# The down projection of a gated MLP: seven products over 14 of 22 k tiles instead of 12, and another order of the last row's tail

## The chip, the cores and the metric

The kernel runs on one core of one Trainium2 chip. The metric is the device time of one execution in microseconds. All arithmetic is in float32: every matrix is split into a high and a low float32r part, and a product of two matrices is three TensorE products (high by high, high by low, low by high), accumulated in PSUM.

## The reference

One decoder block for 512 tokens and 16 meta tokens, model width 1024. Two mixers (an HGRN2 recurrence and a Mamba-2 scan) read one input projection, and one output projection joins them. A gated MLP follows, with a causal convolution of width 3 between the up projection and the activation, and a final RMSNorm:

```python
def conv_glu_ffn(h, w_up, conv_w, conv_b, w_down):
    u = causal_dwconv(h @ w_up, conv_w, conv_b)
    gate, val = jnp.split(u, 2, axis=-1)
    return (jax.nn.silu(gate) * val) @ w_down      # 2816 -> 1024
...
        h = h + conv_glu_ffn(rmsnorm(h, norm2_w[l]), ffn_w_up[l], ...)
    y = rmsnorm(h, final_norm_w)
    return y[:, N_META:, :]
```

The change touches only the last product, `(silu(gate) * val) @ w_down`, and the final norm behind it.

## The kernel before

Activations are held transposed: 128 features on the partitions, tokens along the free axis. The down projection has 22 k tiles (`acs[0..21]`, the gated activations, split into `ah` and `al`) and 8 output row tiles `j` of 128 features, each 512 tokens wide. Row tiles 0 and 1 are plain products (tile `pdn`, lines 1172 to 1174). Row tiles 2 to 7 come in three pairs, `p` = 1, 2, 3, with `j = 2p` and `j2 = 2p + 1`.

Within a pair, `DK` = 6 k tiles from `D0` = 8 on, and the 6 behind them, are multiplied by the scheme of seven products on 2 x 2 blocks: the blocks of the weights are (row j or j2) by (first or second group of k tiles), those of the activations are (group of k tiles) by (first or second 256 tokens). Seven products of `DK` k tiles and 256 columns take the place of eight. The sums of weights that it needs (`sumsdn`) are made by accumulating DMAs on POOL's queue, long before for pairs 1 and 2, and during the plain rows for pair 3. The sums of activations (`gated_sums(i)`: four operations on VectorE, two splits, each of them one on ScalarE and one on VectorE; tiles `g13`, `g24`, then `g0h`, `g0l`, `g1h`, `g1l`) are made while the plain rows run.

The products go by keys, and each has its weight tile of the same name (`whi_d_1` is the high part of a product of pair 1):

- `d0`, `d1`: into `x`, the first 256 tokens of row j. After `d0`, ScalarE copies `x` into `y` (line 1199; PSUM tile `psn2_0`, called `psn` in the trace).
- `d2`: into `y`. Then ScalarE copies `y` into `z`, the second 256 tokens of row j, in the same PSUM tile `pup` as `x` (line 1207).
- `d3`: into `v` (tile `pv`), copied to `ds7` (line 1210).
- `d5` into `z`, `d6` into `y`; `ds7 + z` and `ds7 + y` are then subtracted from row j2.
- `d4`: into `z`.
- The k tiles outside of the scheme, plainly: `qa` (8 tiles) and `qb` (2 tiles) for row j2, `ra` and `rb` for row j; in pair 3 the first half's share is taken earlier as `xa` and `xb`.

Each weight tile goes through three steps: a DMA on SP's queue into `raw`, a ScalarE copy into `whi` (line 203), a VectorE subtraction into `wlo` (line 204). There are three buffers of each. A ScalarE copy waits until TensorE has done with the buffer's tile before. The copies between PSUM tiles stand in the same ScalarE queue.

The order on each engine is set when the program is built, by a scheduler that takes the ready instruction of highest priority in its own estimate of time; `evac()` and `first()` raise priorities, `tc.issue_after` forbids an instruction to stand ahead of another. On the chip, each engine then runs its list in order.

At the end, row 6 (`end`) is finished in halves of 256 tokens: residual added (line 1241), squared (1242), summed over features by two products with a matrix of ones (1245 for the seven earlier rows in `facc`, 1246 for row 6), logarithm and exponential for the reciprocal root (1247, 1248), eight multiplications on VectorE (1253, 1255) and four output DMAs (1257).

Of the kernel before, what the change touches and what calls it, by code (L numbers as in the profile page):

```python
# [43 lines left out]
C_FN = C_FB + 44  # L44
# [8 lines left out]
SPLITS = {7: (0,), 8: (1, 2), 10: (3,), 13: (4,), 15: (5,), 18: (6,), 21: range(7, 22)}  # L53
WS = [j for j in range(KF) if KINDS[j] == "W"]
DN = 1, 2, 3
D0, DK = 8, 6
GROUPS = WS[0:4], WS[4:8], WS[8:12], WS[12:], [("dn", 1), ("dn", 2)], [("dn", 3)]
HT = 258
NUNSC = 5
# [5 lines left out]
def tile_block(ctx: ExitStack, tc: tile.TileContext, xT, w_in, w_dt, w_out, w_up, w_down,  # L65
               par, consts, consti, out, dbg=None):
    nc = tc.nc
    V, A, G, PE = nc.vector, nc.scalar, nc.gpsimd, nc.tensor

    cp = ctx.enter_context(tc.tile_pool(name="cp", bufs=1))  # L70
# [7 lines left out]
    def slot(name, n=NT, dtype=F32, parts=P, tag="m"):  # L78
        return gp.tile([parts, n], dtype, tag=tag, name=name, bufs=TAGS[tag])
# [39 lines left out]
    with first(300000):  # L119
        w = A.activation(warm[:], eps[:], AF.Copy)  # L120
# [47 lines left out]
    chunks += [dn(j, *p) for p in PARTS for j in range(2)]  # L168
    def dn_chunks(p):

        j, j2, c1, c2, c3 = 2 * p, 2 * p + 1, D0 * P, (D0 + DK) * P, (D0 + 2 * DK) * P

        def summed(n):
            return lambda: sumd["dn", p][:, n * DK * P:(n + 1) * DK * P]

        rest = [(("ra", p), w_down[j][:, 0:c1], D0), (("rb", p), w_down[j][:, c3:], KF - D0 - 2 * DK)]
        r = [(("qa", p), w_down[j2][:, 0:c1], D0), (("d0", p), w_down[j][:, c1:c2], DK),
             (("qb", p), w_down[j2][:, c3:], KF - D0 - 2 * DK), (("d1", p), w_down[j][:, c2:c3], DK), (("d2", p), summed(0), DK),
             (("d3", p), summed(2), DK), (("d5", p), summed(1), DK), (("d6", p), w_down[j2][:, c2:c3], DK)]
# [154 lines left out]
    with first(200000):  # L334
        for k in range(0, KD, 2):
            d = slice(k * P, (k + 2) * P)
            for j, w, kx in ((BT, starts[0], k), (CT, starts[1], k + 1)):
                t = slot(f"x{kx}", tag="y")
# [8 lines left out]
        for k in range(KD):  # L347
# [3 lines left out]
            tag = "b0" if k < 4 else "b1"  # L351
# [5 lines left out]
    with first(190000):  # L357
# [18 lines left out]
    with first():  # L376
        for n, (a0, a1) in enumerate(((0, HALF), (HALF, NT))):
            p = bank(f"psn{n}")
# [4 lines left out]
        for k in range(KD):  # L383
            t = slot(f"xn{k}")
# [44 lines left out]
    for n, (a0, a1) in enumerate(((0, HALF), (HALF, NT))):  # L429
        p = bank(f"psd{n}")[0:66, :]  # L430
# [469 lines left out]
    hs, u2h, u2l = [], [], []  # L900
    pos = {}
    acc = None
    for j, s in oorder:
        w = weights("out", j, s)
# [13 lines left out]
        with evac():  # L918
            sq = slot(f"hsq{j}", tag="pr")
# [227 lines left out]
    def partial(ps, w, xs, start=False, stop=False):  # L1147

        for k, (xh, xl) in enumerate(xs):
            wh, wl = (t[:, k * P:(k + 1) * P] for t in w)  # L1150
            one, end = start and k == 0, stop and k == len(xs) - 1
            PE.matmul(ps, wh, xh, start=one, stop=False, skip_group_check=True)  # L1152
            PE.matmul(ps, wh, xl, start=False, stop=False, skip_group_check=True)  # L1153
            PE.matmul(ps, wl, xh, start=False, stop=end, skip_group_check=True)  # L1154
# [31 lines left out]
    whole, K2, KR = slice(0, 512), D0 + DK, D0 + 2 * DK  # L1186
    end = 2 * DN[-1]
    for p in DN:
        j, j2 = 2 * p, 2 * p + 1
        q = bank(f"pq{p}")  # L1190
        partial(q[:], weights("qa", p), gated(0, D0, whole), start=True)
        xz, was = product_banks(True)
        assert was
        other = product_banks(True)[0] if j == end else xz
        x, z, y, v = xz[:, first_half], other[:, 512:768], u1[0][:, first_half], bank(f"pv{p}")[:, first_half]
        sv, s7 = slot(f"dsv{p}", 512, tag="ab"), slot(f"ds7{p}", 256, tag="rs")
# [3 lines left out]
        partial(q[:], weights("qb", p), gated(KR, KF - KR, whole), stop=True)  # L1200
        V.tensor_tensor(hs[j2][:, META:], hs[j2][:, META:], q[:], ALU.add)
        partial(x, weights("d1", p), gated(K2, DK, first_half))
        if j == end:
            partial(x, weights("xb", p), gated(KR, KF - KR, first_half))
        partial(y, weights("d2", p), [t[1] for t in dts])
        with evac():
            A.activation(z, y, AF.Copy)
        partial(v, weights("d3", p), [t[2] for t in dts], start=True, stop=True)
        with evac():
            A.activation(s7[:], v, AF.Copy)  # L1210
# [20 lines left out]
        others(*([] if j == end else [(x, first_half)]), (z, second_half))  # L1231
        if j < end:
            V.tensor_tensor(by_bank(hs[j][:, META:]), by_bank(hs[j][:, META:]), by_bank(xz[:])[:, :, first_half], ALU.add)
            squares(j)
            continue
        hh, halves, ps = hs[j], (0, 256), {0: x, 256: z}
        sq = slot(f"fsq{j}", 512, tag="pr")
        for d0 in halves:
            d, dh = slice(d0, d0 + 256), slice(META + d0, META + d0 + 256)
            with evac():  # L1240
                V.tensor_tensor(hh[:, dh], hh[:, dh], ps[d0], ALU.add)
                A.activation(sq[:, d], hh[:, dh], AF.Square)
                p = bank(f"psn3_{d0}")
                rs = slot(f"rs{d0}", 256, tag="u")
                PE.matmul(p[:, 0:256], ones, acc[:, d], start=True, stop=False)
                PE.matmul(p[:, 0:256], ones, sq[:, d], start=False, stop=True)
                A.activation(rs[:], p[:, 0:256], AF.Ln, bias=eps[:], scale=1.0 / DM)
                A.activation(rs[:], rs[:], AF.Exp, scale=-0.5)
                for k in range(0, KD, 2):
                    ot = slot(f"ot{d0}_{k}", 512, tag="u")[:].rearrange("p (a t) -> p a t", a=2)  # L1250
                    for i in range(2):
                        if k + i == end:
                            V.scalar_tensor_tensor(ot[:, i, :], hh[:, dh], col(C_FN + j), rs[:], ALU.mult, ALU.mult)
                        else:
                            V.tensor_tensor(ot[:, i, :], hs[k + i][:, dh], rs[:], ALU.mult)
                    dst = out[k * P:(k + 2) * P, d].rearrange("(a p) t -> p a t", p=P)
                    (nc.scalar if k % 4 else nc.sync).dma_start(dst, ot)
# [65 lines left out]
```

## Time and profile before

| | |
|---|---|
| median of 3 runs | 864.2 us (863.01 to 865.95) |
| the profiled execution | 863.18 us, its span 861.3 us |
| granted TensorE clock, mean | 0.997 |
| TensorE busy | 842.8 us, 98% of the span |
| VectorE, ScalarE, GpSimd busy | 612.0, 485.9, 117.8 us |
| plain rows 0 and 1 | about 733 to 763 us |
| pairs 1, 2, 3 | about 763 to 792, 792 to 821, 821 to 850.9 us |
| end of the last large product to the end of the span | 850.9 to 861.3 us |

Times in the trace are counted from the span's start. A row of the timeline gives start, duration, engine, line, operation, output<-inputs, and in brackets the idle time ahead of it with what ended it. A TensorE row lasts longer than the distance to the next one, since matmuls overlap; that distance is what one costs. Buffer numbers and the digits in keys are left out in the trace, so all of `whi_d0` to `whi_d6` read `whi_d`.

### The profile page before, as it was taken

How to read it: one execution, taken by the hardware profiler on the slowest of the kernel's cores; microseconds unless marked ns; L12 is line 12 of the kernel's file. 1: busy time of each engine (PE TensorE's matmuls, PEld its weight loads, DVE VectorE, ACT ScalarE, POOL GpSimd, SP SyncE). 2: the span in 40 equal slices, each digit the busy share in tenths (PEclk: the TensorE clock that was granted, in tenths of full speed). 3: DMA queues.
4: the chain of work that ended last, by engine and by line, in shares of the span. 5: the costliest groups of instructions: out<-in, count | busy, mean ns of one | idle time of the engine just before them, and what ended most of it. 6: DMA issues, size and time to landing. Idle time of an engine off the chain costs nothing. (4 is left out here: it accounts for less than half of the span.)

```text
span 861.3 us, 16951 instructions
## 1 busy us (share of the span) xinstructions
PE 842.8 (98%) x6908; PEld 813.4 (94%) x6908; DVE 612.0 (71%) x1040; ACT 485.9 (56%) x777; POOL 117.8 (14%) x156
## 2 busy tenths in 40 slices
PE   7999999999999999999999999999999999999995
PEld 7998899999999999999999999999999999889995
DVE  7983988798766666645244459888888888984544
ACT  8636986867444544454243244567677667663442
POOL 1321022232223131302211220000000000100000
PEclk9999999999999999999999999999999999999998
DMA  7598378893979597957989992355555555945553
GB/s 250 200 250 216 94 253 203 169 152 103 277 141 183 155 281 140 187 145 244 343 164 215 204 168 78 99 171 182 189 190 184 174 177 167 229 114 154 148 150 108
DMA packets 60142, 156.14 MB, mean 181 GB/s; under 512 B 6280, under 2 KB 10760, under 8 KB 60064
## 3 DMA queue, kind: packets, MB, share of 16 engines
q1 hardware_dynamic: 36704, 98.37, 35.0%
q0 software_dynamic: 20832, 53.09, 31.4%
q10 hardware_dynamic: 2528, 3.60, 1.3%
q8 instruction: 54, 0.88, 0.4%
q14 instruction: 24, 0.20, 0.1%
HBM read 152.89 MB, written 55.23 MB: 242 GB/s over the span
## 5 line engine op out<-in xcount | busy, mean ns | idle before, releaser
L326 PE MATMUL pj<-u_hi,whi_in 128*128 128x272 f32 (+1 forms) x752 | 156.6, 288 | 0.0
L326 PE MATMUL pj<-u_lo,whi_in 128*128 128x272 f32 (+1 forms) x752 | 156.6, 287 | 0.0
L326 PE MATMUL pj<-u_hi,wlo_in 128*128 128x272 f32 (+1 forms) x752 | 155.5, 286 | 0.0
L326 PEld LDWEIGHTS pj<-u_hi,whi_in 128*128 128x128 f32 x752 | 115.9, 188 | 2.8 <-issue 2.7
L326 PEld LDWEIGHTS pj<-u_lo,whi_in 128*128 128x128 f32 x752 | 116.0, 188 | 2.4 <-issue 1.8
L326 PEld LDWEIGHTS pj<-u_hi,wlo_in 128*128 128x128 f32 x752 | 116.3, 189 | 1.4 <-issue 1.3
L204 DVE TENSOR_TENSOR wlo_in<-raw_in,whi_in 128x1024 fp32r<-128x1024 f32 (+1 forms) x58 | 64.3, 1108 | 51.2 <-ACT whi_in L203 51.1
L203 ACT ACTIVATE whi_in<-raw_in 128x1024 fp32r<-128x1024 f32 (+1 forms) x58 | 56.0, 966 | 64.1 <-PE pj L326 58.9
L203 ACT ACTIVATE whi_w<-raw_w 128x1024 fp32r<-128x1024 f32 x54 | 57.1, 1058 | 26.4 <-PE pup L1056 13.3
L204 DVE TENSOR_TENSOR wlo_w<-raw_w,whi_w 128x1024 fp32r<-128x1024 f32 x54 | 65.9, 1220 | 6.4 <-ACT whi_w L203 5.8
L221 POOL COPY tick<-ticks 128x1 f32<-128x1 f32 x6 | 9.2, 1537 | 316.0 <-DVE ticks L220 316.0
L1056 PE MATMUL psn<-t1l,whi_w 128*128 128x258 f32 x144 | 40.9, 284 | 0.0
L1057 PE MATMUL pup<-n_hi,wlo_w 128*128 128x258 f32 x144 | 40.7, 283 | 0.1
L1055 PE MATMUL pup<-n_hi,whi_w 128*128 128x258 f32 x144 | 40.8, 283 | 0.0
L1057 PE MATMUL psn<-t1h,wlo_w 128*128 128x258 f32 x144 | 40.7, 282 | 0.0
L1056 PE MATMUL pup<-n_lo,whi_w 128*128 128x258 f32 x144 | 40.6, 282 | 0.0
L204 DVE TENSOR_TENSOR wlo_d<-raw_d,whi_d 128x768 fp32r<-128x768 f32 x21 | 20.1, 957 | 28.7 <-ACT whi_d L203 28.6
L1055 PE MATMUL psn<-t1h,whi_w 128*128 128x258 f32 x144 | 40.4, 280 | 0.0
L241 POOL DMA_DIRECT2D sums<-in_w_up_dram x18 | 21.2, 1179 | 111.2 <-issue 104.9
L204 DVE TENSOR_TENSOR wlo_out<-raw_out,whi_out 128x1024 fp32r<-128x1024 f32 x16 | 19.6, 1225 | 23.5 <-ACT whi_out L203 23.5
L203 ACT ACTIVATE whi_d<-raw_d 128x768 fp32r<-128x768 f32 x21 | 17.8, 847 | 30.7 <-PE pup L1153 14.3
L203 ACT ACTIVATE whi_out<-raw_out 128x1024 fp32r<-128x1024 f32 x16 | 16.9, 1057 | 26.7 <-PE pout L326 16.2
(474 smaller groups left out, 2563.7 us busy)
## 6 DMA issues: line engine op xcount, KB each, us to landing
sums<-in_w_up_dram POOLq DMA_DIRECT2D x54, 512.0 KB, 8.4
raw_in<-in_w_in_dram SPq DMA_DIRECT2D x50, 512.0 KB, 5.4
sums<-in_w_up_dram POOLq DMA_DIRECT2D x36, 256.0 KB, 8.3
raw_w<-in_w_up_dram SPq DMA_DIRECT2D x18, 512.0 KB, 3.5
raw_w<-sums SPq DMA_DIRECT2D x18, 512.0 KB, 3.7
raw_out<-in_w_out_dram SPq DMA_DIRECT2D x16, 512.0 KB, 6.7
sumsdn<-in_w_down_dram POOLq DMA_DIRECT2D x9, 768.0 KB, 8.9
sums<-sums POOLq DMA_DIRECT2D x18, 256.0 KB, 6.8
```

What stands on the lines that cost most here:

```text
L203: A.activation(hi[:, d], raw[:, d], AF.Copy)
L204: eng.tensor_tensor(lo[:, d], raw[:, d], hi[:, d].bitcast(F32), ALU.subtract)
L221: gate = G.tensor_copy(tick[:], ticks[:, n:n + 1])
L241: G.dma_start(ds[j][:, 0:2], of[j][3], accum_op=ALU.add)
L326: PE.matmul(ps[:, O + a0:O + a1], w, x[:, a0:a1], start=s, stop=e)
L1055: PE.matmul(ps, wh, xh, start=first, stop=False, skip_group_check=True)
L1056: PE.matmul(ps, wh, xl, start=False, stop=False, skip_group_check=True)
L1057: last_product[:] = [PE.matmul(ps, wl, xh, start=False, stop=k == H - 1, skip_group_check=True)]
```

## The change

`DK` is 7 instead of 6, so that the scheme takes k tiles 8 to 21, all behind the first 8. `qb`, `rb` and `xb` disappear. `d0` now stands ahead of `qa`. Row j2 gets three subtractions (`ds7` on both halves, then `z` and `y`, each right behind its product) in place of two additions and one subtraction. A seventh `gated_sums` reads `acs[14]` and `acs[21]`; its buffers come from other pools, and `ds7` has one of its own. In the tail, pair 3's `ra` products for the second half are held behind the first half's product of ones with row 6's squares (`normed`).

```diff
-D0, DK = 8, 6
+D0, DK = 8, 7
...
-        if p == DN[-1]:
-            r[6:8] = r[7], r[6]
-            xa, xb = [(key, *rest[n][1:]) for n, key in enumerate((("xa", p), ("xb", p)))]
-            r[4:4], r[9:9] = [xb], [xa]
-        return r + [(("d4", p), summed(3), DK)] + rest
+        last = [(("d4", p), summed(3), DK), (("ra", p), w_down[j][:, 0:c1], D0)]
+        if p == DN[-1]:
+            d5, d6 = d6, d5
+            last.insert(0, (("xa", p), w_down[j][:, 0:c1], D0))
+        return [(("d0", p), w_down[j][:, c1:c2], DK), (("qa", p), w_down[j2][:, 0:c1], D0), (("d1", p), w_down[j][:, c2:], DK),
+                (("d2", p), summed(0), DK), (("d3", p), summed(2), DK), d5, d6] + last
...
-    places = iter(["b1"] * 6 + ["L"] * 4 + ["u"] * 14)
+    places = iter(["b1"] * 6 + ["L"] * 4 + ["u"] * 12 + ["ab", "pr", "u", "pr", "u", "rs"])
...
+        V.tensor_tensor(by_bank(row2), by_bank(row2), s7[:].unsqueeze(1).broadcast_to([P, 2, 256]), ALU.subtract)
         for key in ("d6", "d5") if j == end else ("d5", "d6"):
-            if key == "d5":
-                partial(z, weights(key, p), [t[0] for t in dts])
-            else:
-                partial(y, weights(key, p), [t[3] for t in dts], stop=True)
-        with evac():
-            V.tensor_tensor(sv[:, second_half], s7[:], z, ALU.add)
-            V.tensor_tensor(sv[:, first_half], s7[:], y, ALU.add)
-        V.tensor_tensor(hs[j2][:, META:], hs[j2][:, META:], sv[:], ALU.subtract)
+            ps, n, d = (z, 0, second_half) if key == "d5" else (y, 3, first_half)
+            partial(ps, weights(key, p), [t[n] for t in dts], stop=key == "d6")
+            with evac():
+                V.tensor_tensor(row2[:, d], row2[:, d], ps, ALU.subtract)
...
         if j == end:
             partial(x, weights("xa", p), gated(0, D0, first_half), stop=True)
         partial(z, weights("d4", p), gated(K2, DK, second_half))
...
+            if d0:
+                with tc.issue_after(normed.ins):
+                    partial(z, weights("ra", DN[-1]), gated(0, D0, second_half), stop=True)
             V.tensor_tensor(hh[:, dh], hh[:, dh], ps[d0], ALU.add)
```

What the scheduler makes of it is seen at three places.

TensorE in pair 1, after the change, from the end of `d3` (tile `pv1`) on. `psn2_0` is `y`, `pup0` holds `z`; `g1h_6` and `g1l_6` are of the seventh sums of activations.

```order
L1150 MATMUL pv1_9323<-g0h_6_9134,whi_d3_1_9385 128x256
L1151 MATMUL pv1_9323<-g0l_6_9135,whi_d3_1_9385 128x256
L1152 MATMUL pv1_9323<-g0h_6_9134,wlo_d3_1_9386 128x256
L1150 MATMUL psn2_0_6080<-g1h_6_9138,whi_d2_1_9354 128x256
L1151 MATMUL psn2_0_6080<-g1l_6_9139,whi_d2_1_9354 128x256
L1152 MATMUL psn2_0_6080<-g1h_6_9138,wlo_d2_1_9355 128x256
L1150 MATMUL pup0_6048<-g0h_0_9050,whi_d5_1_9412 128x256
```

The last three products of `d2` stand behind all of `d3`, directly ahead of `d5`. Before the change all of `d2` stands ahead of `d3`:

```order
L1152 MATMUL psn2_0_6080<-g1h_5_9124,whi_d2_1_9368 128x256
L1153 MATMUL psn2_0_6080<-g1l_5_9125,whi_d2_1_9368 128x256
L1154 MATMUL psn2_0_6080<-g1h_5_9124,wlo_d2_1_9369 128x256
L1152 MATMUL pv1_9339<-g0h_0_9050,whi_d3_1_9381 128x256
L1153 MATMUL pv1_9339<-g0l_0_9051,whi_d3_1_9381 128x256
```

Only pair 1 is split in this way; in pairs 2 and 3 `d2` stays whole after the change.

ScalarE in pair 1 around the copy of `y` into `z` (`pup0<-psn2_0`), before:

```order
L1199 ACTIVATE psn2_0_6080<-pup0_6048 128x256
L203 ACTIVATE whi_d3_1_9381<-raw_d3_1_9380 128x768
L203 ACTIVATE whi_d5_1_9405<-raw_d5_1_9404 128x768
L203 ACTIVATE whi_d6_1_9430<-raw_d6_1_9429 128x768
L1207 ACTIVATE pup0_6048<-psn2_0_6080 128x256
L203 ACTIVATE whi_d4_1_9455<-raw_d4_1_9454 128x768
```

One piece of ScalarE's list at the same place, after (`ds71` is the copy of `v`):

```order
L201 ACTIVATE whi_d5_1_9412<-raw_d5_1_9411 128x896
L1176 ACTIVATE facc_9142<-xr0_5235 128x512
L1176 ACTIVATE fsq1_9318<-xr1_5299 128x512
L1177 ACTIVATE xr0_5235<-xr0_5235,pt_75 128x512
L210 ACTIVATE g1h_6_9138<-g24_6_9129 128x512
L1177 ACTIVATE xr1_5299<-xr1_5299,pt_75 128x512
L201 ACTIVATE whi_d6_1_9440<-raw_d6_1_9439 128x896
L1206 ACTIVATE ds71_9324<-pv1_9323 128x256
L201 ACTIVATE whi_d4_1_9469<-raw_d4_1_9468 128x896
L1203 ACTIVATE pup0_6048<-psn2_0_6080 128x256
```

The copy into `z` now stands behind `whi_d6`, `ds71` and `whi_d4`; before it stood behind `whi_d6` alone. In the program after the change, `whi_d6` takes the buffer that `d3`'s tile leaves, and `whi_d4` that of `d2`.

TensorE in the tail, before. `psn3_0` and `psn3_256` are the sums of squares of the two halves, `pup1` is `z` of pair 3.

```order
L1153 MATMUL pup1_6049<-ac1_lo_7288,whi_ra_3_10126 128x256
L1245 MATMUL psn3_0_10212<-facc_9128,cf_76 128x256
L1245 MATMUL psn3_256_10236<-facc_9128,cf_76 128x256
L1154 MATMUL pup1_6049<-ac1_hi_7287,wlo_ra_3_10127 128x256
L1152 MATMUL pup1_6049<-ac2_hi_7291,whi_ra_3_10126 128x256
L1153 MATMUL pup1_6049<-ac2_lo_7292,whi_ra_3_10126 128x256
L1154 MATMUL pup1_6049<-ac2_hi_7291,wlo_ra_3_10127 128x256
L1246 MATMUL psn3_0_10212<-fsq6_10209,cf_76 128x256
L1152 MATMUL pup1_6049<-ac3_hi_7551,whi_ra_3_10126 128x256
```

And after:

```order
L1152 MATMUL pup1_6049<-ac21_hi_9040,wlo_d4_3_10082 128x256
L1235 MATMUL psn3_0_10166<-facc_9142,cf_76 128x256
L1235 MATMUL psn3_256_10214<-facc_9142,cf_76 128x256
L1236 MATMUL psn3_0_10166<-fsq6_10163,cf_76 128x256
L1150 MATMUL pup1_6049<-ac0_hi_7155,whi_ra_3_10113 128x256
```

The three products of ones stand directly behind `d4` (21 products now, 18 before) and ahead of all 24 of `ra`; before, nine of `ra` stood ahead of the last of them, and six of `rb` behind `ra`. VectorE's list still has the first half's eight output multiplications ahead of the second half's residual addition, before and after.

More of the change, by code (lines that the diff above doesn't have):

```diff
@@ L169, in dn_chunks @@
     def dn_chunks(p):
-        j, j2, c1, c2, c3 = 2 * p, 2 * p + 1, D0 * P, (D0 + DK) * P, (D0 + 2 * DK) * P
+        j, j2, c1, c2 = 2 * p, 2 * p + 1, D0 * P, (D0 + DK) * P
         def summed(n):
             return lambda: sumd["dn", p][:, n * DK * P:(n + 1) * DK * P]
[L176 to L179, printed above, removed]
+        d5, d6 = (("d5", p), summed(1), DK), (("d6", p), w_down[j2][:, c2:], DK)
+        last = [(("d4", p), summed(3), DK), (("ra", p), w_down[j][:, 0:c1], D0)]
         if p == DN[-1]:
-            r[6:8] = r[7], r[6]
-            xa, xb = [(key, *rest[n][1:]) for n, key in enumerate((("xa", p), ("xb", p)))]
-            r[4:4], r[9:9] = [xb], [xa]
-        return r + [(("d4", p), summed(3), DK)] + rest
+            d5, d6 = d6, d5
+            last.insert(0, (("xa", p), w_down[j][:, 0:c1], D0))
+        return [(("d0", p), w_down[j][:, c1:c2], DK), (("qa", p), w_down[j2][:, 0:c1], D0), (("d1", p), w_down[j][:, c2:], DK),
+                (("d2", p), summed(0), DK), (("d3", p), summed(2), DK), d5, d6] + last
     for p in DN:
@@ L1185, in tile_block @@
         squares(j)
-    whole, K2, KR = slice(0, 512), D0 + DK, D0 + 2 * DK
+    whole, K2 = slice(0, 512), D0 + DK
     end = 2 * DN[-1]
@@ L1189, in tile_block @@
         j, j2 = 2 * p, 2 * p + 1
-        q = bank(f"pq{p}")
-        partial(q[:], weights("qa", p), gated(0, D0, whole), start=True)
         xz, was = product_banks(True)
@@ L1194, in tile_block @@
         other = product_banks(True)[0] if j == end else xz
-        x, z, y, v = xz[:, first_half], other[:, 512:768], u1[0][:, first_half], bank(f"pv{p}")[:, first_half]
-        sv, s7 = slot(f"dsv{p}", 512, tag="ab"), slot(f"ds7{p}", 256, tag="rs")
+        q, v = bank(f"pq{p}"), bank(f"pv{p}")[:, first_half]
+        x, z, y = xz[:, first_half], other[:, 512:768], u1[0][:, first_half]
+        s7 = cp.tile([P, 256], F32, tag="ds7", name=f"ds7{p}")
+        row, row2 = hs[j][:, META:], hs[j2][:, META:]
         partial(x, weights("d0", p), gated(D0, DK, first_half), start=True)
@@ L1199, in tile_block @@
             A.activation(y, x, AF.Copy)
-        partial(q[:], weights("qb", p), gated(KR, KF - KR, whole), stop=True)
-        V.tensor_tensor(hs[j2][:, META:], hs[j2][:, META:], q[:], ALU.add)
+        partial(q[:], weights("qa", p), gated(0, D0, whole), start=True, stop=True)
+        V.tensor_tensor(row2, row2, q[:], ALU.add)
         partial(x, weights("d1", p), gated(K2, DK, first_half))
-        if j == end:
-            partial(x, weights("xb", p), gated(KR, KF - KR, first_half))
         partial(y, weights("d2", p), [t[1] for t in dts])
@@ L1230, in tile_block @@
         partial(z, weights("d4", p), gated(K2, DK, second_half))
-        others(*([] if j == end else [(x, first_half)]), (z, second_half))
         if j < end:
-            V.tensor_tensor(by_bank(hs[j][:, META:]), by_bank(hs[j][:, META:]), by_bank(xz[:])[:, :, first_half], ALU.add)
+            w = weights("ra", p)
+            for ps, d in ((x, first_half), (z, second_half)):
+                partial(ps, w, gated(0, D0, d), stop=True)
+            V.tensor_tensor(by_bank(row), by_bank(row), by_bank(xz[:])[:, :, first_half], ALU.add)
@@ L1234, in tile_block @@
             squares(j)
-            continue
-        hh, halves, ps = hs[j], (0, 256), {0: x, 256: z}
-        sq = slot(f"fsq{j}", 512, tag="pr")
+    hh, halves, ps = hs[end], (0, 256), {0: x, 256: z}
+    with evac():
+        sq = slot(f"fsq{end}", 512, tag="pr")
         for d0 in halves:
             d, dh = slice(d0, d0 + 256), slice(META + d0, META + d0 + 256)
[L1240 to L1257, printed above, removed]
@@ new lines, in tile_block @@
+            if d0:
+                with tc.issue_after(normed.ins):
+                    partial(z, weights("ra", DN[-1]), gated(0, D0, second_half), stop=True)
+            V.tensor_tensor(hh[:, dh], hh[:, dh], ps[d0], ALU.add)
+            A.activation(sq[:, d], hh[:, dh], AF.Square)
+            p = bank(f"psn3_{d0}")
+            rs = slot(f"rs{d0}", 256, tag="u")
+            PE.matmul(p[:, 0:256], ones, acc[:, d], start=True, stop=False)
+            normed = PE.matmul(p[:, 0:256], ones, sq[:, d], start=False, stop=True)
@@ new lines, in tile_block @@
+            A.activation(rs[:], p[:, 0:256], AF.Ln, bias=eps[:], scale=1.0 / DM)
+            A.activation(rs[:], rs[:], AF.Exp, scale=-0.5)
+            for k in range(0, KD, 2):
+                ot = slot(f"ot{d0}_{k}", 512, tag="u")[:].rearrange("p (a t) -> p a t", a=2)
+                for i in range(2):
+                    if k + i == end:
+                        V.scalar_tensor_tensor(ot[:, i, :], hh[:, dh], col(C_FN + end), rs[:], ALU.mult, ALU.mult)
+                    else:
+                        V.tensor_tensor(ot[:, i, :], hs[k + i][:, dh], rs[:], ALU.mult)
+                dst = out[k * P:(k + 2) * P, d].rearrange("(a p) t -> p a t", p=P)
+                (nc.scalar if k % 4 else nc.sync).dma_start(dst, ot)
```

5 lines of the change are left out of this document (removed).

## The prediction

> **What bounds the kernel now.** I read the page first, then the busy time by stretch, then the chain of waits, then the timeline of each engine around pair 1 and around the end.
>
> ```profile
> span 861.3 us, 16951 instructions
> PE 842.8 (98%) x6908; PEld 813.4 (94%) x6908; DVE 612.0 (71%) x1040; ACT 485.9 (56%) x777; POOL 117.8 (14%) x156
> ...
> 733.00:763.00 30.00, 30.00 (x132) 24.36 (x131) 29.00 (x52) 20.51 (x32) 3.70 (x4) 1.00 0.79 195
> 763.00:792.00 29.00, 29.00 (x219) 27.62 (x218) 17.90 (x28) 14.02 (x22) 0.00 (x0) 1.00 0.46 137
> ...
> 792.81 0.23 PE pq L1153
> 821.69 0.23 PE pq L1153
> ```
>
> TensorE is busy for 98% of the span. In the plain rows (733 to 763; columns are TensorE, weight load, VectorE, ScalarE, GpSimd, clock, DMA share, GB/s) and in pair 1 (763 to 792) it is never idle, so there a product less is time less, and a wait of TensorE is time more. The two rows of the chain are the same place in pairs 2 and 3: one pair takes 28.88 us. Only the last 10 us are not TensorE's; they come below.
>
> **Term 1, the work of TensorE.** In units of a 256-column product, a pair costs 60 for the plain part of row j2 (10 k tiles, three products of 512 columns), 126 in the scheme (7 x 6 x 3) and 60 for the plain part of row j: 246, so 28.88 / 246 = 0.1174 us each. With DK = 7 it is 48 + 147 + 48 = 243. Three units less are 0.35 us a pair. Pairs 1 and 2 give 0.70 us. Pair 3's three units lie behind `xa` and are counted in the tail. Up to the end of `xa` pair 3 has 198 units before and after (before: 60 + 108 + 6 + 24; after: 48 + 126 + 24). This term is small because one more k pair in the scheme saves one block product in eight of it, and nothing else.
>
> **Term 2, a new wait in pair 1.** These are pair 1's rows of ScalarE and TensorE around the copy of `y` into `z` (`pup<-psn`).
>
> ```profile
> 776.28 0.85 ACT L203 ACTIVATE whi_d<-raw_d 128x768 fp32r<-128x768 f32 x1 [1.28 <-PE psn L1153]
> 777.03 0.37 ACT L1207 ACTIVATE pup<-psn 128x256 f32<-128x256 f32 x1
> 778.86 0.85 ACT L203 ACTIVATE whi_d<-raw_d 128x768 fp32r<-128x768 f32 x1 [1.46 <-DMA raw_d<-sumsdn]
> 779.62 0.37 ACT L1210 ACTIVATE ds<-pv 128x256 f32<-128x256 f32 x1
> 780.60 1.06 ACT L203 ACTIVATE whi_ra<-raw_ra 128x1024 fp32r<-128x1024 f32 x1 [0.61 <-PE pup L1154]
> ...
> 776.20 0.28 PE L1152 MATMUL pv<-g0h,whi_d 128*128 128x256 f32 x1
> 778.32 0.28 PE L1152 MATMUL pup<-g0h,whi_d 128*128 128x256 f32 x1
> ```
>
> Before, `d2` ends where `d3` starts, at 776.20. ScalarE starts `whi_d6` 0.08 us later, since it needs `d2`'s buffer, and the copy follows 0.75 us behind it and ends at 777.40. `d5`, which adds to `z`, starts at 778.32. The copy takes 1.20 us, and `d3` covers it with 2.12 us. After, the last three products of `d2` come behind `d3`, and in ScalarE's list the copy stands behind `whi_d6` (which now waits for `d3`), `ds` and `whi_d4`. Let E be the end of `d3`. A `whi` of 896 columns lies midway between 0.85 (768) and 1.06 (1024), 0.95 us, and the next operation follows 0.10 earlier, as above. So `whi_d6` starts at E + 0.08, `ds` at E + 0.93, `whi_d4` 0.30 later (0.37 less the same overlap) at E + 1.23, the copy at E + 2.08, its end is E + 2.45, and TensorE goes on at about E + 2.50. Its own three products end at E + 0.35, and everything behind them in its list is `d5`. It stands still for 2.15 us. The cover that this copy had, `d3`, now lies ahead of it. For bounds: 0 if the copy is on time (rival 1), and 2.6 us if nothing overlaps on ScalarE. If `raw_d` for `whi_d4` lands late, more: before, that operation began at 778.86 and had waited for its DMA. I take 2.15, because each piece is a row of this very place.
>
> Pairs 2 and 3 keep `d2` whole and the copy behind one `whi`: about 0.08 + 0.85 + 0.37 = 1.30 us, under a `d3` of 21 x 0.1174 = 2.47. No wait there.
>
> **Edits that I cost at nothing, and their cover.** The seventh sums of activations are four VectorE operations and two splits, on an engine that is busy 29.0 of 30 us in the plain rows:
>
> ```profile
> 764.83 0.42 DVE L1136 SCALAR_TENSOR_TENSOR g<-g,ac 128x256 f32<-128x256 f32 x1
> 767.04 0.68 DVE L213 TENSOR_TENSOR g0l<-g,g0h 128x512 fp32r<-128x512 f32 x1
> 770.16 0.68 DVE L213 TENSOR_TENSOR g1l<-g,g1h 128x512 fp32r<-128x512 f32 x1
> ...
> L1152 PE MATMUL psn<-g1h,whi_d x36: 277/279/284, 774.1 to 838.5; 128*128 128x256 f32 x36
> ```
>
> Before, the sums end at 770.84 and `d2` needs them at 774.1. After, about 3.0 us (4 x 0.42 + 2 x 0.68) are added, and between them stand two `wlo` of some 1.1 us, an addition to row j2, a square's sum and waits for ScalarE: I get about 777.4 for the last, `g1l_6`. It is wanted where `d3` ends, at about 778.0 (129 units behind the plain rows for 132, 0.35 us earlier than the 778.32 above). Up to 1.2 us of lateness here costs nothing more, since the copy would wait for `whi_d6` and `ds` anyway. The wider `whi`, `wlo` and `raw` tiles (896 for 768) come at longer intervals, since each product key now lasts 2.47 us for 2.12, while VectorE and ScalarE are busy for 17.9 and 14.0 of 29 us in a pair; seven SP loads fall away. The subtractions from row j2 are off TensorE's path; `z` is read behind `d5` and wanted again by `d4`, with all of `d6` between. POOL's sums of weights grow by a sixth; those of pairs 1 and 2 run in a stretch of full DMA queues,
>
> ```profile
> 60.00:70.00 10.00, 10.00 (x82) 1.00 1.05 239
> ```
>
> where TensorE is still busy for all 10 us, and those of pair 3 have some 60 us until they are read. Here I take 0, with up to 1 us as the far end.
>
> **Term 3, the tail.**
>
> ```profile
> 843.81 0.28 PE L1152 MATMUL pup<-ac_hi,whi_d 128*128 128x256 f32 x1
> 846.51 1.02 PE L1245 MATMUL psn<-facc,cf 128*128 128x256 f32 x4
> 847.18 0.47 PE L1154 MATMUL pup<-ac_hi,wlo_ra 128*128 128x256 f32 x1
> 847.49 0.28 PE L1152 MATMUL pup<-ac_hi,whi_ra 128*128 128x256 f32 x1
> 847.84 0.59 PE L1246 MATMUL psn<-fsq,cf 128*128 128x256 f32 x2
> 850.63 0.28 PE L1154 MATMUL pup<-ac_hi,wlo_rb 128*128 128x256 f32 x1
> 853.21 0.70 PE L1246 MATMUL psn<-fsq,cf 128*128 128x256 f32 x2 [2.30 <-ACT fsq L1242]
> ...
> 844.47 0.42 ACT L1242 ACTIVATE fsq<-xr 128x256 f32<-128x256 f32 x1 [0.15 <-DVE xr L1241]
> 848.47 0.47 ACT L1247 ACTIVATE rs<-psn,eps 128x256 f32<-128x256 f32 x1 [3.59 <-PE psn L1246]
> ...
> 849.43 2.10 DVE L1255 TENSOR_TENSOR ot<-xr,rs 128x256 f32<-128x256 f32 x6 [4.66 <-ACT rs L1248]
> 852.18 0.41 DVE L1241 TENSOR_TENSOR xr<-xr,pup 128x256 f32<-128x256 f32 x1
> ```
>
> `xa` ends and `d4` starts at 843.81; call it T. The first half's squares are ready at 844.89, but the product of ones with them starts only at 847.84, T + 4.03, behind 18 + 9 products and the two sums over `facc`. ScalarE follows at 848.47, VectorE's eight outputs at 849.43, and the second half's addition, behind them in VectorE's list, at 852.18 (T + 8.37), although its products end at 850.91. So this chain runs over the first half's outputs, not over the products. The four records of ones cost 847.49 - 846.51 - 0.12 = 0.86 us, two of them 0.43. After: 21 products (2.47) and 0.86, so the product with the squares starts at T + 3.33, 0.70 us earlier, and everything up to the second half's addition with it: T + 7.67. The held `ra` ends at 3.33 + 0.43 + 24 x 0.1174 + 0.16 = T + 6.74, which is 0.9 us ahead of that, so holding it costs nothing; if that cover were gone, its lateness would count in full. The rest is as before. Gain 0.70 us. Bounds: 0 (rival 3), and 1.27 if the products alone ended it (852.18 - 850.91).
>
> **The sum.** -0.70 + 2.15 - 0.70 = +0.75 us: span 862.05, and 863.9 for an execution like the profiled one. That one was 863.18, 1.0 us under the median of 864.2, so against the median I expect 864.9, 0.09% more. A difference of about 0.3%, 2.6 us, is what a measurement of this kernel can tell from no change.
>
> **Rivals.**
>
> 1. *The copy comes in time.* Then only the two gains are left: 864.2 - 1.40 = 862.8. For it, from the list of waits: TensorE waited for copies between PSUM tiles only three times in the whole run, 1.4 us together.
>
> ```profile
> PE pup L1076 <- ACT psn L1062: 0.9, 2, 0.6
> PE pup L1055 <- ACT pup L1062: 0.5, 1, 0.5
> ```
>
> Against it: the list is fixed, and `whi_d4` and `ds` cannot start ahead of `d3`'s end. Chance 0.10. Still within 0.3%.
>
> 2. *The pause lowers TensorE's clock: slower.* The mechanism is one: a stop in pair 1, long enough for the granted clock to fall to a half.
>
> ```profile
> 853.00:854.00 1.00, 0.70 (x2) 1.00 0.99 341
> 854.00:855.00 1.00, 0.00 (x0) 1.00 0.11 37
> 855.00:856.00 1.00, 0.00 (x0) 0.72 0.00 0
> 856.00:857.00 1.00, 0.00 (x0) 0.50 0.41 148
> ...
> 6.16 0.81 PE L326 MATMUL pj_b<-v_hi,whi_in 128*128 128x272 f32 x2 [6.16 <-ACT v_hi L353]
> 11.61 0.64 PE L326 MATMUL pj_b<-v_hi,whi_in 128*128 128x272 f32 x2
> 12.05 0.54 PE L326 MATMUL pj_c<-v_hi,whi_in 128*128 128x272 f32 x2
> 12.67 0.41 PE L326 MATMUL pj_b<-v_hi,wlo_in 128*128 128x272 f32 x2
> 12.92 0.40 PE L326 MATMUL pj_c<-v_lo,whi_in 128*128 128x272 f32 x2
> ```
>
> At the start, two products take 0.44 us (11.61 to 12.05) until about 12.2, and 0.25 (12.67 to 12.92) from then on; 6 us of slow products lose 6 x (1 - 0.25/0.44) = 2.6 us. With that, 864.9 + 2.6 = 867.5, 0.4% slower. Against it: at the end, TensorE idles for 2.30 us (850.91 to 853.21) and the clock still reads 1.00; it falls at about 855.7, after 4.8 us with 0.7 us of work in them. A stop of 2.15 is shorter than the one that left the clock alone; the point from which it decides is between the two, some 3 to 4 us, and a late `raw_d` could bring it there. Chance 0.09. The Trainium skill, "TensorE: Matmul & The Clock Gate", under "What's actually happening" in Part 1, says that the clock halves after at least one idle window of about 3.4 us in a free-running count, and comes back after a busy one. By that rule a stop of 2.15 us leaves the clock whole and the sum stands; if it fired, one window at half speed would lose an estimated 1.7 us in place of the 2.6. The trace agrees in that 2.30 us did not lower it.
>
> 3. *The tail gives nothing*, if something else holds the first half (its squares' sum over seven rows, a buffer for row 6's squares out of a pool that now has two fewer): 864.9 + 0.7 = 865.6. Against it: the wait of 3.59 us ahead of `rs` was for TensorE alone. Chance 0.07.
>
> 4. *The larger sums of weights disturb the loads* between 40 and 80 us and TensorE waits there: 1 to 3 us, up to 868. The row at 60 us, with no idle time, speaks against it. Chance 0.04.
>
> **How the numbers follow.** My forecast has the other 0.70, and gives 864.9. The range leaves out most of rivals 2 and 4 at the top, and at the bottom goes a little below rival 1, for the scatter of 863.0 to 866.0 among the runs before: 862.3 to 867.2. Slower by over 0.3% takes most of rivals 2 and 4 and a late `raw_d`: 0.12. Faster by over 0.3% needs more than the two gains and their far ends together (1.40 + 0.57 = 1.97 us of 2.6), so only scatter: 0.05. The same: 0.83.
>
> **What would show it.** In the profile after: a stop of TensorE of about 2.1 us in pair 1, ahead of the first `d5` product, ended by the copy `pup<-psn` on ScalarE (line 1203 there), which starts about 2.1 us after `d3`'s end; none in pairs 2 and 3; from pair 2's first product to pair 3's, 28.53 us; the first half's `rs` 4.0 us behind `d4`'s start (4.66 before); a clock of 1.00 up to the end. It is wrong if the stop is missing or is ended by `g1l`, by `raw_d` or by the clock, or if TensorE waits in the first 100 us.

## The result, and the profile after

The median is 868.9 us over 22 runs (864.89 to 874.54), against 863.31 us for the kernel before over 22 runs: a ratio of 1.0054, 95% interval 1.0038 to 1.007. The forecast was 864.9 us and at most 867.2. The profiled execution of the changed kernel is one of the shorter ones, 865.79 us with a span of 863.8; the longer ones have a lower mean clock (0.997 in the run of 864.89 us, 0.990 in that of 874.54), so part of the loss is not to be seen in this one trace.

The head of the page, and the list of TensorE's waits (line waited at, releaser, us in total, times, longest), both of the kernel after:

```profile
span 863.8 us, 16935 instructions
PE 842.9 (98%) x6917; PEld 813.7 (94%) x6917; DVE 615.0 (71%) x1039; ACT 485.5 (56%) x772; POOL 117.9 (14%) x156
...
PE pup L1150 <- ACT pup L1203: 2.0, 1, 2.0
PE psn L1236 <- ACT fsq L1232: 1.9, 1, 1.9
...
PE psu L583 <- ACT btk L557: 0.8, 1, 0.8
```

TensorE is busy for as long as before (842.9 us for 842.8) in a span that is 2.5 us longer. The first row is the stop that was forecast. The last, 0.8 us at 83 us, stood before as

```profile
PE psu L585 <- ACT btk L559: 0.4, 1, 0.4
```

The timeline of TensorE and ScalarE in pair 1 after the change:

```profile
778.62 0.28 PE L1150 MATMUL psn<-g1h,whi_d 128*128 128x256 f32 x1
781.08 0.39 PE L1150 MATMUL pup<-g0h,whi_d 128*128 128x256 f32 x1 [1.96 <-ACT pup L1203]
...
778.70 0.95 ACT L201 ACTIVATE whi_d<-raw_d 128x896 fp32r<-128x896 f32 x1 [0.84 <-PE pv L1151]
779.55 0.37 ACT L1206 ACTIVATE ds<-pv 128x256 f32<-128x256 f32 x1
779.82 0.94 ACT L201 ACTIVATE whi_d<-raw_d 128x896 fp32r<-128x896 f32 x1
780.65 0.38 ACT L1203 ACTIVATE pup<-psn 128x256 f32<-128x256 f32 x1
```

This is the chain of term 2, step by step: `d3` ends where `d2`'s last three products start, at 778.62; `whi_d6` starts 0.08 later, then `ds`, `whi_d4`, and the copy at 2.03 behind `d3`'s end (2.08 forecast). The trace has 1.96 us of idle time; counted as the prediction counts, from the end of `d2`'s three products by their distance of 0.118 us, the stop is 781.08 - 778.62 - 0.35 = 2.11 us for 2.15. In this execution the clock reads 1.00 all around it.

The tail, from TensorE's, ScalarE's and VectorE's timelines (`d4` starts at 846.3):

```profile
849.66 0.59 PE L1236 MATMUL psn<-fsq,cf 128*128 128x256 f32 x2
855.03 1.08 PE L1236 MATMUL psn<-fsq,cf 128*128 128x256 f32 x2 [1.95 <-ACT fsq L1232]
...
850.29 0.48 ACT L1237 ACTIVATE rs<-psn,eps 128x256 f32<-128x256 f32 x1 [2.90 <-PE psn L1236]
...
853.99 0.42 DVE L1231 TENSOR_TENSOR xr<-xr,pup 128x256 f32<-128x256 f32 x1
```

The product of ones with the first half's squares starts 3.35 us behind `d4` (3.33 forecast), `rs` 4.0 behind it, the second half's addition 7.7. Up to there the tail does what term 3 says. In this execution the gain does not reach the end: the last product of ones takes 1.08 us for 0.70 before, since the clock fell to 0.50 at about 855.2, and from `d4`'s start to the end of the span are 17.5 us before and after.

### The profile page after: what moved, and what is told of

Read it like the earlier page. It is cut to its first block, busy times and chain, and to the rows that moved or that the text cites. A ratio compares the mean times of both kernels' runs of the same rounds, so it can differ in the third digit from the quotient of the medians.

```text
span 863.8 us, 16935 instructions
## 1 busy us (share of the span) xinstructions
PE 842.9 (98%) x6917; PEld 813.7 (94%) x6917; DVE 615.0 (71%) x1039; ACT 485.5 (56%) x772; POOL 117.9 (14%) x156
## 5 line engine op out<-in xcount | busy, mean ns | idle before, releaser
L201 ACT ACTIVATE whi_d<-raw_d 128x896 fp32r<-128x896 f32 x21 | 20.0, 952 | 33.4 <-PE pup L1151 14.8
L202 DVE TENSOR_TENSOR wlo_d<-raw_d,whi_d 128x896 fp32r<-128x896 f32 x21 | 22.9, 1091 | 11.9 <-ACT whi_d L201 11.7
```

The lines of the kernel that those rows point to most:

```text
L201: A.activation(hi[:, d], raw[:, d], AF.Copy)
L202: eng.tensor_tensor(lo[:, d], raw[:, d], hi[:, d].bitcast(F32), ALU.subtract)
```

## Experiments

**What does the stop cost, and is it all?** Four kernels ran beside each other (before: 863.79 us median). The first is the changed kernel once more.

> The changed kernel once more, for a trace of one of its longer executions (868 us or more). Theory A, the clock: the stop of TensorE in pair 1 (1.96 us in the first trace) lets the granted clock fall to a half in most executions, each time for 3 to 10 us; a trace of a longer execution shows a stretch of granted clock 0.50 that starts within 4 us of the stop, products at about 0.23 us for 0.117 in it, and nothing longer anywhere else; its mean clock is 0.990 to 0.994 for 0.995 to 0.997. Theory B, the loads: the sums of weights, larger by a sixth, delay loads in some executions; then the added time lies at waits of TensorE or ScalarE for DMAs, at 40 to 80 us or in the plain rows, at a clock of 1.00. Median 866 to 870 by both.

Measured: 870.75 us, ratio 1.0062 (1.0042 to 1.0083). The loss is there again. The profiled execution is again one of the shorter ones, 867.21 us, with the same stop of 1.96 us at a clock of 1.00 and waits of 0.7 us (`psu`) and 0.6 us (`psx`) between 83 and 95 us; theory A's stretch at 0.50 is not in it. So no trace shows the changed kernel in a run of 869 us or more; what such a run loses is inferred below from its variants.

The second takes the stop out: in pair 1, `whi_d6`, `ds` and `whi_d4` are held behind the copy (the `whi` are issued behind `hold[0]`).

```diff
...
-            A.activation(z, y, AF.Copy)
+            zc = A.activation(z, y, AF.Copy)
+        hold[:] = [zc] if p == 1 else []
...
-        with evac():
+        with evac(), tc.issue_after(zc.ins):
             A.activation(s7[:], v, AF.Copy)
...
```

> The change with one more order: in pair 1 the copy of y into z stands ahead of whi_d6, ds and whi_d4 on ScalarE. The stop of TensorE should shrink from 1.96 to about 0.5 us (0.08 + 0.37 + 0.05 behind the last product of d2). Theory A: with so short a stop the clock stays whole, the spread of several us goes, and the time is 863.3 - 1.4 + 0.5 = 862.4, 0.1% under the kernel before. Theory B: the loads are the same, so the time only falls by the 1.5 us that the stop loses, to about 867, and the spread stays.

Measured: 865.76 us, ratio 1.0019 (0.9997 to 1.0041). The stop shrank to 0.5 us, and some 3 to 5 us came back, more than the 1.5 us of stop. Neither expectation came (862.4 or about 867): the kernel is still not at the 862 us that the gains alone would give. Its list of waits and the busy time from 60 to 200 us (columns as before: TensorE, weight load, VectorE, ScalarE, GpSimd, clock, DMA share, GB/s) show what else there is:

```profile
PE psu L586 <- ACT btk L560: 2.2, 1, 2.2
PE pup L1153 <- ACT pup L1206: 0.5, 1, 0.5
...
80.00:90.00 10.00, 7.79 (x39) 5.79 (x39) 3.86 (x7) 6.69 (x23) 0.00 (x0) 0.83 0.83 286
```

The wait of 0.4 us at 83 us is now one of 2.2 us, and the granted clock of the 10 us around it is 0.83, though nothing was edited there.

The third puts a stop alone into the kernel before: eleven copies of `y` into a scratch tile ahead of the copy `y` to `z`, and the same three instructions behind it.

> The kernel before, with eleven copies of 256 columns into an unused tile ahead of the copy of y into z in pair 1 (nothing else; whi_d6, ds and whi_d4 behind the copy). TensorE should stop for about 11 x 0.27 - 0.87 = 2.1 us at the place where the changed kernel stops. Theory A: 863.3 + 2.1 and the clock on top: 866 to 870, with a spread of several us and mean clocks down to 0.991. Theory B: 863.3 + 2.1 = 865.4 and no more spread than before (0.5%).

Measured: 867.82 us, ratio 1.0036 (1.0022 to 1.0049), with a stop of 2.79 us. By the medians it costs 4.0 us, more than its length. The profile shows the rest as clock:

```profile
781.22 0.39 PE L1155 MATMUL pup<-g0h,whi_d 128*128 128x256 f32 x1 [2.79 <-ACT pup L1215]
...
782.00:786.00 4.00, 4.00 (x24) 4.00 (x24) 2.25 (x3) 1.99 (x3) 0.00 (x0) 0.62 0.30 64
```

The fourth is the kernel before with the last row's second half held, and nothing else:

```diff
-            others(*([] if j == end else [(x, first_half)]), (z, second_half))
...
+                if d0:
+                    with tc.issue_after(normed.ins):
+                        others((z, second_half))
```

> The kernel before with the second part of the change alone: pair 3's ra and rb products of the second half held behind the first half's product of ones with the squares. That product then starts at T + 18 x 0.1174 + 0.86 = T + 2.97 for T + 4.03, and all behind it comes 1.06 us earlier: about 862.2 by both theories, and no stop in pair 1, no more spread than before.

Measured: 862.28 us, ratio 0.9976 (0.9965 to 0.9987). The tail is a gain by itself, of 1.5 us by the medians, where 1.06 had been worked out for `d4` with 18 products.

**Is it the sums of weights?** The letters change from here on. Theory A now says that the larger sums delay a load, that TensorE pauses for it and that the clock falls with the pause. Rival B says in the next run that the sums are hidden, and in the later ones that the stop of pair 1 is the whole loss. The sums are the only thing that the change touches ahead of 500 us: `sumsdn` of pairs 1 and 2 has 896 columns for 768. In the kernel before, only that was widened; TensorE's, ScalarE's and SyncE's lists stay as they were. (The products then read other columns than they should, so this kernel's output is not the block's.)

```diff
...
-                c, w = D0 * P, DK * P
+                c, w = D0 * P, (DK + (j[1] != 3)) * P
```

> The kernel before with only the sums of pairs 1 and 2 widened from 768 to 896 columns at their old place (the products read 768 of them, of other columns than they should, so the output of the down projection differs; every instruction but the DMAs of the sums stays). Theory A: the loads ab land in 7 to 8 us for 5.2, ScalarE waits for them, TensorE waits 0.8 to 2.2 us for btk at 83 us, and the median rises by 1.5 to 3 us with a wider spread: 865 to 867 us. Rival B (the larger sums are hidden): as before, 863.3 to 864 us.

Measured: 866.76 us against 863.77, ratio 1.0038 (1.0021 to 1.0055). Rival B falls. Here is the way that it takes, first before, then after, then in this kernel: from the table of DMAs (KB of each, median us from issue to landing), ScalarE's timeline and TensorE's.

```profile
ab<-acum_d SPq DMA_DIRECT2D x8, 264.0 KB, 5.2
...
81.51 1.47 ACT L611 ACTIVATE L<-ab,acm 128x2 f32<-128x2 f32 x5 [4.22 <-DMA ab<-acum_d]
...
83.18 1.12 PE L585 MATMUL psu<-xdc,btk 16*128 16x512 f32 x2 [0.40 <-ACT btk L559]
```

```profile
ab<-acum_d SPq DMA_DIRECT2D x8, 264.0 KB, 8.3
...
81.81 1.46 ACT L609 ACTIVATE L<-ab,acm 128x2 f32<-128x2 f32 x5 [4.62 <-DMA ab<-acum_d]
...
83.48 1.12 PE L583 MATMUL psu<-xdc,btk 16*128 16x512 f32 x2 [0.80 <-ACT btk L557]
```

```profile
ab<-acum_d SPq DMA_DIRECT2D x8, 264.0 KB, 8.0
...
85.56 1.46 ACT L612 ACTIVATE L<-ab,acm 128x2 f32<-128x2 f32 x5 [7.94 <-DMA ab<-acum_d]
...
87.23 2.07 PE L586 MATMUL psu<-xdc,btk 16*128 16x512 f32 x2 [4.12 <-ACT btk L560]
...
84.00:88.00 4.00, 0.77 (x1) 0.50 (x2) 0.00 (x0) 2.37 (x9) 0.00 (x0) 0.78 1.01 281
88.00:92.00 4.00, 4.00 (x12) 2.26 (x11) 1.30 (x3) 4.00 (x14) 0.00 (x0) 0.50 0.94 364
...
86.00:87.00 1.00, 0.00 (x0) 0.00 (x0) 0.00 (x0) 1.00 (x5) 0.00 (x0) 0.61 1.04 264
```

The decays `ab` are loaded on SP's queue from about 77 us on. The sums share the DMA engines with them, and in all three kernels their last DMAs run into that time. The last one is issued at 72.78, 76.70 and 78.93 us and lands 6.1, 8.3 and 10.2 us later: before, only its end met the decays, and in the other two it runs beside them for 5 us and more. With a sixth more bytes the decays land some 3 us later. ScalarE meets them in its list ahead of the copy `btk` and waits; TensorE needs `btk`. Before, 4.2 us of ScalarE's wait were nearly all covered (0.40 us came through). Everything beyond comes through one for one. In the third kernel the clock falls at about 86.2 us, a microsecond before the pause of 4.12 us ends, and stays at half until 93.0: 5.8 us of work at half speed. This trace is of the longest run of that kernel, 870.16 us.

**Where else can the sums go?** Two places failed, and tell something. Behind unit 8 of the up projection, at about 612 to 658 us:

> The changed kernel with one thing moved: the sums of the weights of pairs 1 and 2 (POOL's queue, issued from 32 us on) are issued behind unit 8 of the up projection, at about 620 us, where POOL has nothing to issue. Theory A (the sums, a sixth larger, delay the decays' loads ab at 77 to 85 us; ScalarE waits for them ahead of the copy btk, TensorE for btk, and the granted clock falls behind such a pause): the waits of psu and psx between 60 and 100 us go (0.4 us or less), the loads ab land in about 4 us instead of 8.3, the long runs of 870 us and more go, and the median is the one before with the pairs' -0.7, the tail's -1.5 and the stop's +2 to +3: 863 to 865 us. Rival B (the stop of pair 1 and the clock behind it cost it all): as the changed kernel, 868.5 to 871 us, with the same stop of 2.0 us.

> The changed kernel with the sums of pairs 1 and 2 at about 620 us, and in pair 1 the copy y to z ahead of whi_d6, ds and whi_d4 on ScalarE. Theory A: neither the early pause nor more than 0.5 us of the stop is left, so the pairs' -0.7 and the tail's -1.5 remain: 861 to 862 us, with runs within 1 us of each other. Rival B (the stop alone): as with the copy first alone, 865 to 866 us.

> The kernel before with the sums of pairs 1 and 2 (768 columns) issued behind unit 8 at about 620 us. Theory A: the pause of 0.4 us at 83 us goes, and with it some of the longer runs of 865 to 867: 862.8 to 863.5 us against 863.5. If the move itself saved more than that (2 us and over), what the two kernels with late sums gain over the changed one would not be the larger sums' doing but that of the early place for any sums; if it costs (the sums now beside the up projection's loads), it is over 864.

Measured: 880.86, 877.86 and 874.19 us. The early pause is gone in all three (TensorE busy for all 40 us from 60 to 100), but the control loses 10 us by itself, so none of them tells the two theories apart. The median landing of the control's loads and sums between 600 and 670 us, behind the same loads of the kernel before, and its longest new wait:

```profile
raw_w<-in_w_up_dram SPq DMA_DIRECT2D x7, 512.0 KB, 4.0
```

```profile
raw_w<-in_w_up_dram SPq DMA_DIRECT2D x6, 512.0 KB, 10.8
sumsdn<-in_w_down_dram POOLq DMA_DIRECT2D x6, 768.0 KB, 10.8
...
PE pup L1054 <- ACT pup L1061: 3.8, 4, 2.6
```

Next, with the up projection's first sums, from 118 us on:

> The kernel before with the sums of the weights of pairs 1 and 2 (768 columns) issued with the first group of the up projection's sums (from 118 us), so that both run to about 215 us, where the queues had been at 0.39 of their time; at 620 us they cost 10 us, since the up projection's loads came late. Theory A: the loads between 60 and 100 us are undisturbed, no wait of psu; 862.5 to 863.6 us against 863.6 (the 0.4 us at 83 us and some longer runs). Rival: the sums take 2 us and more wherever they stand, since loads of the projections come late there as well: over 865.5.

> The changed kernel with the sums of pairs 1 and 2 issued from 118 us with the first group of the up projection's. Theory A (half and more of the loss is the early pause and the clock behind it): the pause at 83 us is gone, the stop of 2.0 us in pair 1 stays with its clock: 863.5 to 866 us, less than the changed kernel by 3 to 5. Rival B (the stop and the clock behind it are the loss): 868.5 to 871 us.

> The changed kernel with the sums of pairs 1 and 2 from 118 us and, in pair 1, the copy y to z ahead of whi_d6, ds and whi_d4. Theory A: what is left are the pairs' -0.7, the tail's -1.5 and 0.5 us of stop: 861 to 862.3 us and a spread under 2 us. Rival B: 865 us and over, as with the copy first alone.

> The kernel before (12 of 22 tiles by seven products) with the sums of pairs 1 and 2 from 118 us and the last row's second half held. If 14 tiles save their 0.7 us once both waits are gone, this is 0.2 us (0.7 less 0.5 of a stop) above the version with 14 tiles and the copy first: 861 to 862.5 us. If 14 tiles cost something besides the two waits, it is faster than that version by 1 us and more.

Measured: 873.86, 879.95, 880.21 and 873.26 us. Again the control loses 10 us. All later sums are pushed back (the third group's gate from 296 to 306 us), so that those of the second group now run beside the HGRN heads' load `rb`. From the control's table of DMAs between 285 and 320 us and its timelines:

```profile
rb<-rs_d SPq DMA_DIRECT2D x4, 257.0 KB, 8.3
...
305.34 0.75 DVE L877 SCALAR_TENSOR_TENSOR o<-o,pt,rb 128x514 f32<-128x514 f32 x1 [3.85 <-DMA rb<-rs_d]
307.38 0.14 DVE L838 COPY_PREDICATED mt<-maskA,pm 16x2 f32<-16x2 int32 x1
...
307.57 0.59 PE L851 MATMUL pm<-mt 128*128 128x2 f32 x2 [10.34 <-DVE mt L838]
```

Before the change `rb` landed in 4.1 us there. VectorE waits four times for `rb` there, 14.8 us together (5.4 before). It is the same pattern as at 83 us: a load that the sums slow, an engine that meets it in its list (VectorE here) ahead of something short that TensorE needs, and a pause of 10.34 us.

**The early pause taken out cleanly.** Pair 1's sums stay at 32 us, and pair 2's go behind unit 0 of the up projection, at 518 us, where POOL has nothing left to issue and the DMA engines are 0.2 to 0.3 busy. TensorE's, ScalarE's and SyncE's lists stay the same.

```diff
-GROUPS = ..., [("dn", 1), ("dn", 2)], [("dn", 3)]
+GROUPS = ..., [("dn", 1)], [("dn", 2)], [("dn", 3)]
...
-        if j == 20:
-            weight_sums(GROUPS[5], ac)
+        if j in (0, 20):
+            weight_sums(GROUPS[5 + j // 20], ac)
```

> The changed kernel with the sums of pair 1 alone at their old place (from 32 us) and those of pair 2 behind unit 0 of the up projection (from 518 us, where the queues were at 0.22 to 0.34 of their time). TensorE's, ScalarE's and SyncE's orders are those of the changed kernel. Theory A (the early pause and the clock behind it): the loads ab land in about 4 us, no wait of psu; the stop of 2.0 us stays: 863.5 to 866 us, 3 to 5 less than the changed kernel. Rival B (the stop and its clock alone): 868.5 to 871. Rival C (also at 518 us the sums delay the up projection's loads): a new wait of pup there and over 870.

> The same with, in pair 1, the copy y to z ahead of whi_d6, ds and whi_d4. Theory A: 861 to 862.3 us and a spread under 2 us (pairs -0.7, tail -1.5 to -2, early wait -0.4, a stop of 0.5). Rival B: 865 to 866, as with the copy first alone. Rival C: over 868.

> The kernel before with the same split of the sums (768 columns). Theory A: the wait of 0.4 us at 83 us goes: 862.8 to 863.6 against 863.6. Rival C: over 866.

> The kernel before with the split of the sums and the last row's second half held: 861 to 862 us by theory A. Against the version with 14 tiles and the copy first it says what two more tiles by seven products are worth when neither wait is there: 0.2 us by the prediction's terms (0.70 less a stop of 0.5).

Measured, beside 863.69 us for the kernel before:

| kernel | median, us | ratio (95%) |
|---|---|---|
| after, sums split | 865.63 | 1.0023 (1.0011 to 1.0035) |
| after, sums split, copy first | 863.30 | 0.9993 (0.9983 to 1.0003) |
| before, sums split | 863.12 | 0.9992 (0.9981 to 1.0002) |
| before, sums split, tail held | 862.05 | 0.9976 (0.9966 to 0.9987) |

In the first of them `ab` lands in time and the pause is gone:

```profile
79.48 1.47 ACT L609 ACTIVATE L<-ab,acm 128x2 f32<-128x2 f32 x5 [1.81 <-DMA ab<-acum_d]
...
83.09 1.12 PE L583 MATMUL psu<-xdc,btk 16*128 16x512 f32 x2
```

So the changed kernel's loss has two parts: 868.9 - 865.63 = 3.3 us went with the early pause, and 865.63 - 863.30 = 2.3 us with the stop of pair 1 (1.5 us of it is its own length, 1.96 less 0.46; the rest, 0.8, I put down to the clock). The first size compares two series: by their ratios to the kernel before it is (1.0054 - 1.0023) x 863 = 2.7 us, and the sums widened alone cost 3.0. Rivals B and C fall. What is left of the change, at 863.30, is no gain on the kernel before; 861 to 862.3 had been expected. The best version is the last row, and it has 12 tiles; against the kernel before with the tail alone (862.28) the split of the sums is within the scatter. 14 tiles cost 1.25 us there instead of gaining 0.2.

## Why the prediction was wrong

**The step that failed first: "Edits that I cost at nothing", POOL's sums.** I took 0, with 1 us as the far end, and looked for an effect in one row, 60 to 70 us, with no idle time. The row was right (TensorE is busy for those 10 us after the change too), but it was the wrong place. The last DMA of the sums is issued at 72.8 us before the change and at 76.7 after it, and what it delays is the load that starts there, at about 77 us. The sign was in the list of waits before, 0.40 us at `psu`, ended by ScalarE, which itself had waited 4.22 us for `ab`: a chain with no cover left. I had not followed that wait back. This is rival 4; I named it, with about the right size (1 to 3 us), the wrong stretch (40 to 80 us) and a chance of 0.04. The wait of 0.40 us was the reason to give it more. A wait of TensorE in the first 100 us was also one of the signs by which the prediction said it would be wrong.

**Rival 2, the clock.** Its mechanism holds and its deciding point is wrong. I put that between 3 and 4 us, since 2.30 us of idle time at the end of the kernel left the clock alone. (The fall after it was at about 855.4, not 855.7: a mean of 0.72 over that microsecond is 0.44 us at full clock and 0.56 at half.) The runs have shorter pauses that lowered it. These are the changed kernel with the sums split, where the same stop of 1.96 us as in the trace above was followed by this (the stop is from 778.72 to 780.68):

```profile
781.50:782.00 0.50, 0.50 (x5) 0.50 (x4) 0.48 (x1) 0.00 (x0) 0.00 (x0) 0.50 0.71 136
...
784.00:785.00 1.00, 1.00 (x7) 1.00 (x6) 0.07 (x1) 0.28 (x1) 0.00 (x0) 0.55 0.80 283
```

Half the clock from 781.5 to 784.9, 3.4 us, which is 1.7 us of work lost; in the changed kernel's own profiled execution the same stop cost no clock. Five traces hold this stop of 1.96 us. Three show a clock of 0.50 for 3.4 us after it: this one, the changed kernel with the sums at 614 us (TensorE resumes at 796.90) and the one with the sums from 118 us on (796.36). The two of the changed kernel itself do not. With the sums at 614 us, a pause of 1.77 us (up to 298.29) lowered it as well and one of 2.30 us (up to 644.09) did not, so in this range the length alone does not decide it. Three fifths of 1.7 us are 1.0 us a run, near the 0.8 of the medians. Whether such a pause pays is then, as far as these traces go, a matter of the execution: the price comes as a chance in each run, not as a threshold. It is only part of the spread of 864.9 to 874.5: with the stop alone (sums split) the runs reach 868.5, with the early pause alone (copy first) 873.5. The 1.7 us is also the estimate that the Trainium skill's window gives ("TensorE: Matmul & The Clock Gate", "What's actually happening" in Part 1: a free-running window of about 3.4 us), and the trace agrees in the 3.4 us. It does not agree that the window must be idle: 1.96 us of idle time were enough here.

**Term 2, right.** 2.11 us for 2.15 by the distance between the products, by the steps named; none in pairs 2 and 3. Of the price of a late copy I had only the length.

**Term 1, too large.** Pair 2's first product to pair 3's measured 28.66 us (`pq` from 796.82 to 825.48 after; 28.65, from 794.25 to 822.90, with both waits gone), against 28.53 forecast and 28.88 before: 0.23 us for 0.35. One price for all units, 28.88 / 246 = 0.1174, is a small part of the error. By the distances in the timeline of the kernels with 14 tiles and the sums split, a unit in a 512-column product costs 0.1156 us and one in a 256-column product 0.1184; the change takes away twelve of the cheap ones and adds nine of the dear ones, which still makes 1.39 - 1.07 = 0.32. The other 0.09 is a dearer 256-column unit: (28.65 - 48 x 0.1156) / 195 = 0.1185 after, (28.88 - 60 x 0.1156) / 186 = 0.1180 before. Why it is dearer stays open. With both waits gone, pair 1 takes 29.35 us with a stop of 0.62 in it (0.46 of idle time in the trace), so 28.73 without it.

**Term 3, right in its steps.** All times from `d4`'s start to the second half's addition came to 0.02 us; behind it, in the changed kernel's own trace, the clock took 0.4 us of the 0.70 back and 0.3 more lies behind the last output multiplication. With the sums split and the copy first, where the last product of ones took 0.70 us, `d4`'s start to the end is 16.8 us for 17.5 before. In the kernel before, the held half is worth 1.1 to 1.5 us by the medians (863.12 to 862.05, 863.79 to 862.28), where `d4` has 18 products for 21 and 1.06 had been worked out; in the traces it is 1.06 us, as the second pair of rows below shows against 115.46 us before (732.38 to 847.84). From the first plain product to the first half's product of ones, with 14 tiles and both waits gone, and with 12 tiles and the tail held:

```profile
731.88 0.39 PE L1173 MATMUL pdn<-ac_hi,whi_dn 128*128 128x512 f32 x1
847.08 0.59 PE L1241 MATMUL psn<-fsq,cf 128*128 128x256 f32 x2
```

```profile
731.51 0.39 PE L1172 MATMUL pdn<-ac_hi,whi_dn 128*128 128x512 f32 x1
845.91 0.59 PE L1249 MATMUL psn<-fsq,cf 128*128 128x256 f32 x2
```

115.20 us against 114.40. With 12 tiles `rb` is held too (30 units for 24), so the tail's gain does not need the 14. The other 0.4 us of the 1.25 between these two kernels lie ahead of the down projection (first plain product at 731.88 for 731.51) and are no larger than what two kernels with the same program up to there differ by (731.19 in the trace with the split alone).

**The sum.** The terms gave +0.75; with the stop at 0.62 they would give -0.78, and the trace of the kernel with both waits gone has 115.20 less 115.46, -0.26. So 0.5 us of the gain was not there, all of it in the pairs: without the stop, pairs 1 and 2 gave 0.31 for 0.70, and pair 3 up to the end of `xa` took 23.32 us for 23.20. The larger error is in the two costs around it: about 3 us of an early pause taken as 0, and 0.8 us of clock on the stop taken as 0.

## What to carry to other kernels

When an edit makes a background transfer larger, follow back each short wait of the bounding engine in the stretch where that transfer ends, to the load behind it: a wait of 0.4 us says that the cover is used up, and the next microsecond will come through in full. A pause of the bounding engine is to be priced at its length plus a chance of the clock's window, and a run's mean clock and the spread between executions show whether it is paid. Moving a transfer to "a free place" needs its own control: here two of three places cost 10 us.

## What the runs showed of the hardware

- Pauses of 1.77, 2.21 and 2.79 us, and three of five pauses of 1.96 us, were each followed by 3.4 us at a clock of 0.50, beginning 0.1 to 1.2 us after TensorE had resumed. In one of 4.12 us the clock fell 3.1 us after the pause began and stayed at 0.50 for 6.8 us. The other two pauses of 1.96 us and one of 2.30 us left it at 1.00.
- Sums that accumulate in DRAM slow a load of 512 KB beside them from 4.0 to 10.8 us, with the DMA share at 0.96 to 1.05 (620 to 660 us) for 0.55 to 0.58 before.
- On TensorE, two 256-column products cost 2.4% more than one of 512 columns (0.1184 for 0.1156 us a unit, with 14 tiles and the sums split), so that a unit count across shapes is not a time.
